# Attention by whole blocks of 128 queries instead of halves of 64, in a fused sliding-window trunk

## Chip, cores and metric

One core of one Trainium2 chip. The metric is the device time of one execution in microseconds (us), median of several runs. One execution is also recorded by the hardware profiler; its spans are measured from its first instruction.

Engines: PE is TensorE (matmul), DVE is VectorE, ACT is ScalarE, POOL is GpSimd, SP is SyncE, which issues most DMAs. PEld is PE's loading of stationary operands.

## What is computed

One layer of a trunk on 512 tokens of width 2048: an RMS norm, attention in a sliding window of 128 keys (32 heads of 64, 4 key/value heads, a relative bias by head, a sink per head in the softmax), a gate, the output projection, then a gated embedding and a last norm. In the reference, cut to the attention:

```python
qi, kj = np.arange(BLOCK)[:, None], np.arange(2 * BLOCK)[None, :]
dist = qi + BLOCK - kj
band = (dist >= 0) & (dist < WINDOW)
scores = einsum('bnqhgd,bnjhd->bnhgqj', q, kb) * HEAD_DIM ** -0.5 + bias
scores = where(mask, scores, finfo.min)
m = maximum(scores.max(-1), sink)
e = exp(scores - m)
probs = e / (e.sum(-1) + exp(sink - m))
out = einsum('bnhgqj,bnjhd->bnqhgd', probs, vb)
y = (out * silu(gate)) @ w_out
x = x + y
x = x + (p @ ple_proj) * sigmoid(rmsnorm(x) @ ple_gate)
return rmsnorm(x, final_g)
```

## The kernel before

Everything is float32 to the eye. To run PE at the rate of its reduced float32 (`F32R`) without losing digits, each operand is split into a high part (a cast on ACT) and a low part (a subtraction on DVE), and a product is three matmuls: high by high, high by low, low by high (`mm3`, L125 to L130).

The kernel has four stages. Up to about 72 us it loads x and the first weights and makes keys, values and the first two pairs of query heads. Then come the **projections** for the other queries and for the gates, 30 pieces ("kinds", L182 to L192) of 16 steps; a step is one `mm3`, three matmuls of 128 x 512. Attention is woven between these steps. From 453 us the output projection and the gated embedding follow, each by a seven-product scheme on quadrants. The last stretch has no matmul.

Attention goes over 8 groups of four heads (`TWOS`, index d) and, in each, over 8 **halves** of 64 queries (`UNITS`, index g); i counts the 64 of these. The 128 rows of a score tile are 4 heads by 32 queries, so a half needs two score products (u = 0, 1). Three functions, written as generators, hold a half's steps:

- `scores(i)` (L447): two products of Q with the keys (L463) into a PSUM tile `s` of two banks, 160 keys wide, high and low part of the key side by side; POOL puts the sink into the row; DVE adds the bias and the two parts (L488, L489), folds the keys that two of the rows don't share (L490) and takes the maxima (L492); ACT takes the exponentials and their sums (L496); DVE inverts the sums (L498); ACT scales (L507) into `pr`.
- `turn(i)` (L509): two transposes (L516) into a bank `pt`; ACT and DVE split it into high and low (L521, L522), which are `r`; from the second block of queries on POOL cuts out the triangle of the window (L532), and ACT puts the low part beside the high one (L542): `own`.
- `weigh(i)` (L544): two products with V (L558) and, from the second block on, one of `own` with differences of V (L560) into a bank `o`, which two halves share; after the second half ACT and DVE add its two parts into `u` (L569, L571).

The loop over i (L824) sets the order. In this stage no scheduler moves an instruction: PE, SP, DVE, ACT and POOL take them as written (L329). At the head of iteration i stand the transposes of half i-2, the products with V of half i-3 and the scores of half i, then about seven projection steps. Between these steps stand the later parts of the generators and **chores**: the splits of the next weights (`W.todo`, one slot an iteration; L111 on ACT, L112 on DVE), the evacuation of a finished projection (`evac_q`, L305, with splits L320 and L322; `open_gate`, L589), the splits of the next key (`make_key`, L341), the gating of finished heads (`gate_value`, L582), the triangles' differences (`first_chores`, L428). Two more DMA chains run through it: `sum_weights` (L641) has SP copy and POOL add blocks of later weights in DRAM, and `load_bias` (L439) fetches the next bias.

`q_at` (L182) places the queries' projections so that Q of group d is ready for half 8 d. PSUM has eight banks: two each for projections ("p"), `pt` ("t") and `o` ("o"), and one buffer of two banks for `s`.

Of the kernel before, what the change touches and what calls it, by code (L numbers as in the profile page):

```python
# [11 lines left out]
F32 = mybir.dt.float32  # L12
# [18 lines left out]
UNITS = S // HB  # L31
# [9 lines left out]
WARM = 24  # L41
PAD = 48
# [14 lines left out]
def trunk_kernel(ctx: ExitStack, tc: tile.TileContext, a: dict):  # L57
# [11 lines left out]
    others = {"s": banks_s.enter_context(tc.tile_pool(name="psum_s", bufs=2, space=PSUM))}  # L69
# [112 lines left out]
    q_at = {int(0.5 + 3.516 * (c // 2)) - 3 + c % 2: c for c in range(2, PAIRS)}  # L182
# [214 lines left out]
    spsum = mid.enter_context(tc.tile_pool(name="psum_w", bufs=1, space=PSUM))  # L397
# [7 lines left out]
    U, T, PT, O, gates, biases = {}, {}, {}, {}, {}, {}  # L405
# [41 lines left out]
    def scores(i):  # L447

        d, g = divmod(i, UNITS)
        if g == 4 and d + 1 < TWOS:
            load_bias(d + 1)
        key = K[d // 2]

        s_ps = spsum.tile([P, 2, S], F32, tag="w", name=f"s{i}")
        number = [min(2 * g + u + 1, 5) * QB for u in range(2)]
        for u in range(2):  # L460
            first, n = max(2 * g + u - 4, 0) * QB, number[u]
            st = Q[d][:, 2 * g + u].rearrange("p h q -> p (h q)")
            nc.tensor.matmul(s_ps[:, u, : 2 * n], st, key[:, :, first : first + n], start=True, stop=True)  # L463
        W = KEYS + 2
        t = apool.tile([P, 2, W], F32, tag="t", name=f"t{i}", bufs=3)
        at = t[:, 0, 0:1]

        def two(of, stride, n):
            return bass.AP(tensor=at.tensor, offset=at.offset + of, ap=[at.ap[0], [stride, 2], [1, n]])

        late = QB if g >= 2 else 0
        seen = [t[:, 0, 0 : P + 1], t[:, 1, 1 + late : P + 2 + late] if late else t[:, 1, 0 : P + 1]]
        both = two(0, W + 1 + late if late else W, P + 1)
        pr = [t[:, u, 1 + late * u : 1 + late * u + P] for u in range(2)]
        nc.gpsimd.tensor_copy(two(0, W + W - 1 if late else W, 1), sinkb[:, d : d + 1].unsqueeze(1).to_broadcast([P, 2, 1]))
        for u, n in enumerate(number):
            if n < P:
                nc.gpsimd.memset(t[:, u, 1 + n : 1 + P], MASKED)
        yield
        bias = biases[d][:, ::-1]  # L480
        if g < 2:
            for u, n in enumerate(number):
                nc.vector.tensor_add(t[:, u, 1 : 1 + n], s_ps[:, u, :n], bias[:, KEYS - n :])
            for u, n in enumerate(number):
                nc.vector.tensor_add(t[:, u, 1 : 1 + n], s_ps[:, u, n : 2 * n], t[:, u, 1 : 1 + n])
        else:
            x = t[:, :, 1 : 1 + KEYS]
            nc.vector.tensor_add(x, s_ps[:, :, :KEYS], bias.unsqueeze(1).to_broadcast([P, 2, KEYS]))  # L488
            nc.vector.tensor_add(x, s_ps[:, :, KEYS : 2 * KEYS], x)  # L489
            nc.vector.tensor_max(two(1, W + P, QB), t[:, :, 1 : 1 + QB], t[:, :, 1 + P : 1 + KEYS])  # L490
        sm = apool.tile([P, 24], F32, tag="sm", name=f"sm{i}", bufs=4)
        nc.vector.tensor_reduce(sm[:, 0:2], both, axis=AX.X, op=ALU.max, negate=True)  # L492
        yield
        for u in range(2):
            su = seen[u]
            nc.scalar.activation(su, su, AF.Exp, bias=sm[:, u : u + 1], accum_out=sm[:, 2 + u : 3 + u])  # L496
        yield
        nc.vector.reciprocal(sm[:, 4:6], sm[:, 2:4])  # L498
        yield

        T[i] = apool.tile([P, 2, P], F32, tag="pr", name=f"pr{i}", bufs=3)
        for u in range(2):
            out, src = T[i][:, u], pr[u]
            if late and (g + u) % 2:
                out = out.rearrange("p (h k) -> p h k", h=2)[:, ::-1]
                src = src.rearrange("p (h k) -> p h k", h=2)
            nc.scalar.mul(out, src, sm[:, 4 + u : 5 + u])  # L507

    def turn(i):  # L509


        d, g = divmod(i, UNITS)
        pr = T.pop(i)
        pt = bank(f"pt{i}", "t")[:, :256]
        for u in range(2):
            nc.tensor.transpose(pt[:, u * P : (u + 1) * P], pr[:, u, :], ident)  # L516

        r = apool.tile([P, 2, 256], F32R, tag="r", name=f"r{i}", bufs=2)
        rh, rl = (r[:, l].rearrange("p (h u q) -> p u h q", h=4, u=2) for l in range(2))
        src = pt.rearrange("p (u h q) -> p u h q", u=2, h=4)  # L520
# [3 lines left out]
        own = None  # L524
        if g >= 2:
            own = apool.tile([P, 2, 256], F32R, tag="own", name=f"own{i}", bufs=2)
            rows = slice(0, P) if g % 2 else slice(0, HB)
            flat = lambda v: v[rows].rearrange("p l (u q) -> p (l u) q", q=HB)


            sign = -1 if g % 2 else 1
            nc.gpsimd.affine_select(  # L532
                out=flat(own), in_=flat(r).bitcast(F32), pattern=[[0, 8], [sign, HB]], compare_op=ALU.is_ge, fill=0.0,
                base=-HB - 1 if g % 2 else 0, channel_multiplier=-sign,
            )
        PT[i] = (r, own)
        yield
        if own is not None:
            here, there = slice(HB, P), slice(0, HB)
            if g % 2 == 0:  # L540
                here, there = there, here
            nc.scalar.copy(own[there, 0], own[here, 1].bitcast(F32))  # L542

    def weigh(i):  # L544

        d, g = divmod(i, UNITS)
        n, b = divmod(g, 2)
        kv = d // 2
        r, own = PT.pop(i)
        if g == 0:  # L550
            U[d] = apool.tile([P, 2, S], F32, tag="u", name=f"u{d}", bufs=3)
        if b == 0:
            O[d] = bank(f"o{i}", "o").rearrange("p (b u e q) -> p b u e q", b=2, u=2, e=2)
        ops = O[d]
        out = ops[:, b].rearrange("p u e q -> p (u e q)")
        first = V[0 if n == 0 else n - 1 + b][:, kv]
        for low in range(2):
            nc.tensor.matmul(out, first, r[:, low], start=low == 0, stop=own is None and low == 1)  # L558
        if own is not None:
            nc.tensor.matmul(  # L560
                out, DV[:, n - 1, b, kv * 2 * HD : (kv + 1) * 2 * HD], own[:, 0], start=False, stop=True
            )
        yield
        if b:
            dst = U[d][:, :, n * P : (n + 1) * P].rearrange("p u (b q) -> p b u q", b=2)
            lower, upper = slice(0, 64), slice(64, 128)
            tmp = [apool.tile([P, 2, 2, HB], F32, tag=f"tmp{e}", name=f"tmp{e}_{i}", bufs=1) for e in range(2)]
            for e, (o, x) in enumerate(((lower, upper), (upper, lower))):
                nc.scalar.copy(tmp[e][o], ops[x, :, :, e, :])  # L569
            for e, o in enumerate((lower, upper)):  # L570
                nc.vector.tensor_add(dst[o], ops[o, :, :, e, :], tmp[e][o])  # L571
        if g == UNITS - 1:
# [243 lines left out]
    blocks = TWOS * UNITS  # L816
# [6 lines left out]
    softmax = iter(())  # L823
    for i in range(blocks + 3):  # L824
# [476 lines left out]
```

## Time and profile before

| what | value |
|---|---|
| median of 3 runs | 798.1 us (797.66 to 798.22) |
| the profiled execution, its own time | 798.39 us |
| its span, first to last instruction | 796.4 us |
| PE busy | 786.1 us |
| DVE, ACT, POOL busy | 586.9, 500.5, 117.4 us |
| mean granted clock of PE | 0.997 |

How to read it: a line of a group gives the source line, engine, operation, what is written from what, the shape, the count, and behind the bar the busy time, the mean duration of one in ns, and the idle time ahead of these instructions with what ended it. A line of the order in time gives start and duration in us. A matmul's duration reaches to the end of its result, and the next one starts before that; so durations of PE overlap, and its pace is read from starts. PE's weight load before each matmul is a row of its own (PEld).

### The profile page before, as it was taken

What the parts mean: (1) busy time and instruction counts of PE and PEld (TensorE: products, weight loads), DVE (VectorE), ACT (ScalarE), POOL (GpSimd) and SP (SyncE); (2) the same over time, 40 slices, a digit from 0 to 9 for tenths busy, and PEclk for the clock granted to TensorE, in tenths of its full rate; (3) what the DMA queues carried; (4) which work ended last, traced back from release to release, by engine and by line L of the source; (5) the groups of instructions that cost most, each with busy time, mean ns of one, the idle gap of its engine ahead of it and who ended that gap; (6) DMA issues with size and microseconds to landing.
All of it is one profiled execution on the core that took longest, in us unless ns stands there. A gap on an engine that the chain in (4) does not pass through costs nothing.

```text
span 796.4 us, 10979 instructions
## 1 busy us (share of the span) xinstructions
PE 786.1 (99%) x3758; PEld 658.4 (83%) x3758; DVE 586.9 (74%) x1026; ACT 500.5 (63%) x1057; POOL 117.4 (15%) x238
## 2 busy tenths in 40 slices
PE   9999999999999999999999999999999999999995
PEld 8888888888888888888888888888888888888884
DVE  4555697877878687777778898766646757988896
ACT  6652576666767586666657645555568656656765
POOL 0030223131212213121222100030000020200000
PEclk9999999999999999999999999999999999999998
DMA  9882389697869869777965478997613995787633
GB/s 352 260 243 92 113 261 236 174 255 179 223 178 255 204 192 241 188 220 171 260 156 150 118 267 328 356 256 235 204 34 103 374 212 197 155 225 220 206 106 106
DMA packets 42919, 165.28 MB, mean 208 GB/s; under 512 B 6048, under 2 KB 7072, under 8 KB 39024
## 3 DMA queue, kind: packets, MB, share of 16 engines
q1 hardware_dynamic: 35456, 129.67, 47.6%
q0 software_dynamic: 7408, 34.93, 23.6%
q8 instruction: 29, 0.48, 0.2%
q14 instruction: 26, 0.21, 0.1%
HBM read 157.70 MB, written 46.19 MB: 256 GB/s over the span
## 4 chain that ended last, share of the span: by engine, by line
PE 99%; DVE 0%; ACT 0%; issue 0%; ACTq 0%; DVEq 0%
PE gps L128 7%; PE gps L130 7%; PE gps L129 7%; PE qps L128 7%; PE qps L130 7%; PE qps L129 7%; PE o L128 6%; PE o L130 6%; PE o L129 6%; PE g L128 5%; PE g L129 5%; PE g L130 5%; PE s L463 2%; PE o L558 2%; PE vps L280 2%; PE pt L516 2%
## 5 line engine op out<-in xcount | busy, mean ns | idle before, releaser
L676 DVE TENSOR_TENSOR blo<-braw,bhi 128x1024 fp32r<-128x1024 f32 x80 | 97.7, 1221 | 40.0 <-ACT bhi L675 40.0
L675 ACT CAST bhi<-braw 128x1024 fp32r<-128x1024 f32 x80 | 84.1, 1052 | 65.6 <-PE g L130 21.7
L128 PE MATMUL gps<-xh,whi 128*128 128x512 f32 x256 | 99.9, 390 | 0.1
L130 PE MATMUL gps<-xh,wlo 128*128 128x512 f32 x256 | 99.8, 390 | 0.0
L129 PE MATMUL gps<-xl,whi 128*128 128x512 f32 x256 | 99.8, 390 | 0.0
L128 PE MATMUL o<-bhi,fho 128*128 128x512 f32 x224 | 87.7, 391 | 0.0
L128 PE MATMUL qps<-xh,whi 128*128 128x512 f32 x224 | 87.7, 391 | 0.0
L130 PE MATMUL qps<-xh,wlo 128*128 128x512 f32 x224 | 87.4, 390 | 0.0
L129 PE MATMUL qps<-xl,whi 128*128 128x512 f32 x224 | 87.4, 390 | 0.0
L129 PE MATMUL o<-blo,fho 128*128 128x512 f32 x224 | 87.2, 389 | 0.0
L130 PE MATMUL o<-bhi,flo 128*128 128x512 f32 x224 | 87.2, 389 | 0.0
L112 DVE TENSOR_TENSOR wlo<-wraw,whi 128x1024 fp32r<-128x1024 f32 x60 | 73.8, 1231 | 2.8 <-ACT whi L111 2.4
L128 PE MATMUL g<-bhi,fhg 128*128 128x512 f32 x192 | 75.1, 391 | 0.0
L130 PE MATMUL g<-bhi,flg 128*128 128x512 f32 x192 | 74.8, 389 | 0.0
L129 PE MATMUL g<-blo,fhg 128*128 128x512 f32 x192 | 74.7, 389 | 0.0
L532 POOL TENSOR_SCALAR_AFFINE_SELECT own<-r 64x512 fp32r<-64x512 f32 (+1 forms) x48 | 32.4, 675 | 254.8 <-DVE r L522 250.1
L521 ACT CAST r<-pt 128x256 fp32r<-128x256 f32 x64 | 23.8, 371 | 71.8 <-PE pt L516 71.5
L522 DVE TENSOR_TENSOR r<-pt,r 128x256 fp32r<-128x256 f32 x64 | 27.1, 423 | 55.7 <-ACT r L521 55.0
L111 ACT CAST whi<-wraw 128x1024 fp32r<-128x1024 f32 x60 | 62.3, 1040 | 5.3 <-issue 3.9
L676 DVE TENSOR_TENSOR blo<-grown,bhi 128x1024 fp32r<-128x1024 f32 x32 | 39.1, 1223 | 23.6 <-ACT bhi L675 23.4
L130 PEld LDWEIGHTS gps<-xh,wlo 128*128 128x128 f32 x256 | 48.1, 188 | 10.1
L128 PEld LDWEIGHTS gps<-xh,whi 128*128 128x128 f32 x256 | 48.1, 188 | 9.4 <-PE vps L280 0.5
(207 smaller groups left out, 1739.7 us busy)
## 6 DMA issues: line engine op xcount, KB each, us to landing
wraw<-in_w_gate_in SPq DMA_DIRECT2D x32, 512.0 KB, 5.5
wraw<-in_w_q SPq DMA_DIRECT2D x28, 512.0 KB, 4.6
w_out<-in_w_out POOLq DMA_DIRECT2D x24, 512.0 KB, 7.2
braw<-in_w_out SPq DMA_DIRECT2D x24, 512.0 KB, 4.3
braw<-in_ple_gate SPq DMA_DIRECT2D x24, 512.0 KB, 4.4
xw<-in_first SPq DMA_DIRECT2D x14, 640.5 KB, 6.4
w_out<-in_w_out SPq DMA_DIRECT2D x16, 512.0 KB, 6.0
ple_gate<-in_ple_gate SPq DMA_DIRECT2D x16, 512.0 KB, 6.7
```

Source lines behind the costliest of these rows:

```text
L111: nc.scalar.copy(hi, raw)
L112: nc.vector.tensor_sub(lo, raw, hi.bitcast(F32))
L128: nc.tensor.matmul(ps, sh, mh, start=first, stop=False, skip_group_check=more)
L129: nc.tensor.matmul(ps, sh, ml, start=False, stop=False, skip_group_check=more)
L130: nc.tensor.matmul(ps, sl, mh, start=False, stop=last, skip_group_check=more)
L280: nc.tensor.matmul(v_ps[t], h[:, c], both[:, :, 256:512], start=f, stop=e, skip_group_check=True)
L463: nc.tensor.matmul(s_ps[:, u, : 2 * n], st, key[:, :, first : first + n], start=True, stop=True)
L521: nc.scalar.copy(rh, src)
L522: nc.vector.tensor_sub(rl, src, rh.bitcast(F32))
L532: nc.gpsimd.affine_select(out=flat(own), in_=flat(r).bitcast(F32), pattern=[[0, 8], [sign, HB]], compare_op=ALU.is_ge, fill=0.0, base=-HB ...
L675: nc.scalar.copy(hi, raw)
L676: nc.vector.tensor_sub(lo, raw, hi.bitcast(F32))
```

## The change

The unit of attention becomes a block n of 128 queries: 32 units instead of 64. `scores` makes four products into a PSUM tile of four banks, and each DVE step of the softmax (adds, fold, maxima, reciprocals) and the split of the transposes is one instruction for four rows of heads instead of two. Exponentials, scalings, transposes, triangles, and the products with V are as many as before and of the same shapes. Four transposes go to one whole bank. In the first block of each group of heads the eight adds of narrow shapes stay apart.

The loop runs 34 times. At the head of iteration j stand, in this order, the scores of block j, the products with V of block j-2, the transposes of block j-1; then 13 or 14 projection steps, in two sevens (`HALF`) that carry the chores as an iteration did before. `t` and `o` lose their second bank, which `s` takes. The buffers of `pr`, `r`, `own` go from three, two, two to one of twice the size, `t` from three to two. `q_at` changes its step from 3.516 to 3.41, since 34 iterations divide the projections otherwise than 66; the first projection woven in is now a query piece.

```diff
-    others = {"s": banks_s.enter_context(tc.tile_pool(name="psum_s", bufs=2, space=PSUM))}
+    others = dict.fromkeys("sto", banks_s.enter_context(tc.tile_pool(name="psum_s", bufs=2, space=PSUM)))
...
-    q_at = {int(0.5 + 3.516 * (c // 2)) - 3 + c % 2: c for c in range(2, PAIRS)}
+    q_at = {int(0.5 + 3.41 * (c // 2)) - 3 + c % 2: c for c in range(2, PAIRS)}
...
-    spsum = mid.enter_context(tc.tile_pool(name="psum_w", bufs=1, space=PSUM))
+    spsum = mid.enter_context(tc.tile_pool(name="psum_w", bufs=1, space=PSUM, reuse_waits="tile"))
+    others.update(dict.fromkeys("to", spsum))
...
-        s_ps = spsum.tile([P, 2, S], F32, tag="w", name=f"s{i}")
-        number = [min(2 * g + u + 1, 5) * QB for u in range(2)]
-        for u in range(2):
-            first, n = max(2 * g + u - 4, 0) * QB, number[u]
-            st = Q[d][:, 2 * g + u].rearrange("p h q -> p (h q)")
-            nc.tensor.matmul(s_ps[:, u, : 2 * n], st, key[:, :, first : first + n], start=True, stop=True)
+        s_ps = spsum.tile([P, 4, S], F32, tag="w", name=f"s{i}")
+        number = [min(4 * n + v + 1, 5) * QB for v in range(4)]
+        for v in range(4):
+            first, c = max(4 * n + v - 4, 0) * QB, number[v]
+            st = Q[d][:, 4 * n + v].rearrange("p h q -> p (h q)")
+            nc.tensor.matmul(s_ps[:, v, : 2 * c], st, key[:, :, first : first + c], start=True, stop=True)
         W = KEYS + 2
-        t = apool.tile([P, 2, W], F32, tag="t", name=f"t{i}", bufs=3)
+        t = apool.tile([P, 4, W], F32, tag="t", name=f"t{i}", bufs=2)
...
-            nc.vector.tensor_add(x, s_ps[:, :, :KEYS], bias.unsqueeze(1).to_broadcast([P, 2, KEYS]))
+            nc.vector.tensor_add(x, s_ps[:, :, :KEYS], bias.unsqueeze(1).to_broadcast([P, 4, KEYS]))
             nc.vector.tensor_add(x, s_ps[:, :, KEYS : 2 * KEYS], x)
-            nc.vector.tensor_max(two(1, W + P, QB), t[:, :, 1 : 1 + QB], t[:, :, 1 + P : 1 + KEYS])
+            pairs = t.rearrange("p (b u) c -> p b u c", u=2)
+            nc.vector.tensor_max(four(1, W + P, QB), pairs[:, :, :, 1 : 1 + QB], pairs[:, :, :, 1 + P : 1 + KEYS])
...
-        nc.vector.reciprocal(sm[:, 4:6], sm[:, 2:4])
+        nc.vector.reciprocal(sm[:, 8:12], sm[:, 4:8])
...
-        T[i] = apool.tile([P, 2, P], F32, tag="pr", name=f"pr{i}", bufs=3)
+        T[i] = apool.tile([P, 4, P], F32, tag="pr", name=f"pr{i}", bufs=1)
...
-        pt = bank(f"pt{i}", "t")[:, :256]
-        for u in range(2):
-            nc.tensor.transpose(pt[:, u * P : (u + 1) * P], pr[:, u, :], ident)
-
-        r = apool.tile([P, 2, 256], F32R, tag="r", name=f"r{i}", bufs=2)
+        pt = bank(f"pt{i}", "t")
+        for v in range(4):
+
+            c = 2 * (v % 2) + v // 2
+            nc.tensor.transpose(pt[:, c * P : (c + 1) * P], pr[:, v, :], ident)
+        yield
+
+        r = apool.tile([P, 2, 512], F32R, tag="r", name=f"r{i}", bufs=1)
...
-        if b == 0:
-            O[d] = bank(f"o{i}", "o").rearrange("p (b u e q) -> p b u e q", b=2, u=2, e=2)
...
+        ops = bank(f"o{i}", "o").rearrange("p (b u e q) -> p b u e q", b=2, u=2, e=2)
+        for b in range(2):
+            out = ops[:, b].rearrange("p u e q -> p (u e q)")
+            first = V[0 if n == 0 else n - 1 + b][:, kv]
+            for low in range(2):
+                nc.tensor.matmul(
+                    out, first, r[:, low, 256 * b : 256 * b + 256], start=low == 0, stop=not n and low == 1
+                )
+            if n:
+                nc.tensor.matmul(
+                    out, DV[:, n - 1, b, kv * 2 * HD : (kv + 1) * 2 * HD], own[b][:, 0], start=False, stop=True
+                )
...
-    for i in range(blocks + 3):
...
+    for j in range(blocks + 2):
+
+        softmax = scores(j) if j < blocks else iter(())
+        turned = turn(j - 1) if 1 <= j <= blocks else iter(())
+        value = weigh(j - 2) if 2 <= j else iter(())
+        for part in (softmax, value, turned, softmax, turned):
+            next(part, None)
+        todo = left // (blocks + 2 - j)
         left -= todo
-        for n in range(max(todo, 6)):
+        for n in range(max(todo, 2 * HALF)):
+            h, at = divmod(n, HALF)
+            i = 2 * j + h
             if n < todo:
                 next(proj)
...
+            for part in {1: (turned,), 3: (softmax,), 5: (softmax, value), 6: (softmax,), 8: (turned,)}.get(n, ()):
+                next(part, None)
+            if at == HALF - 1 and h < 2 and j < blocks:
+                sums(i)
```

162 lines of the change are left out of this document (69 added, 93 removed).

## The prediction

> **What bounds the kernel now.** I read the page first: which engine is full, and when. Then the busy times by stage, which say whether the attention stage has any gap on TensorE that could be won.
>
> ```profile
> span 796.4 us, 10979 instructions
> PE 786.1 (99%) x3758; PEld 658.4 (83%) x3758; DVE 586.9 (74%) x1026; ACT 500.5 (63%) x1057; POOL 117.4 (15%) x238
> ```
>
> ```profile
> core 0: us, PE busy (x) PEld busy (x) DVE busy (x) ACT busy (x) POOL busy (x), PEclk, DMA share, GB/s
> 83.00:453.00 370.00, 370.00 (x1825) 311.23 (x1825) 284.78 (x625) 248.35 (x678) 80.84 (x173) 1.00 0.75 202
> ```
>
> Attention lies between about 83 and 453 us, interleaved with the projections. There PE is busy for 370.00 of 370.00 us at a granted clock of 1.00; DVE has 285 and ACT 248. So PE's stream of products sets the time, and DVE and ACT have 85 and 122 us to spare. What they save is worth nothing by itself; it only buys slack.
>
> The Trainium skill ("Perfetto Trace Analysis", "Identifying the Most-Contended Engine") says that matmul busy time is no good measure of PE's headroom, since matmuls are pipelined, and looks at weight loads instead; those stand at 311 of 370 us here. By that rule a full PE row is no proof. So I check the pace itself, on the order of PE's instructions in time (start, duration):
>
> ```profile
> 255.22 0.38 PE L516 MATMUL pt<-ident,pr 128*128 128x128 f32 x2
> 255.35 0.48 PE L558 MATMUL o<-r,V 128*128 128x256 f32 x2
> 255.67 0.28 PE L560 MATMUL o<-own,DV 128*128 128x256 f32 x1
> 255.79 0.46 PE L463 MATMUL s<-k,q 128*128 128x320 f32 x2
> 256.09 0.39 PE L128 MATMUL gps<-xh,whi 128*128 128x512 f32 x1
> 256.32 0.40 PE L129 MATMUL gps<-xl,whi 128*128 128x512 f32 x1
> 256.55 0.39 PE L130 MATMUL gps<-xh,wlo 128*128 128x512 f32 x1
> 256.78 0.39 PE L128 MATMUL gps<-xh,whi 128*128 128x512 f32 x1
> ...
> 260.64 0.39 PE L130 MATMUL gps<-xh,wlo 128*128 128x512 f32 x1
> 260.87 0.38 PE L516 MATMUL pt<-ident,pr 128*128 128x128 f32 x2
> ```
>
> Starts count here, since durations overlap. From 256.78 to 260.64 are 17 long products: 0.227 us each. One half (two transposes, three products with V, two scores) takes 256.09 - 255.22 = 0.87. From one half to the next are 260.87 - 255.22 = 5.65 us, and 0.87 + 21 x 0.227 = 5.64. So the whole price of a change between short and long products is what is left: 0.013 us a half, with rounded starts anything from 0.00 to 0.02. It is seen where it should be: the three long products after a half take 0.69 (256.09 to 256.78) for 0.68, the last before the next 0.23 for 0.227.
>
> **The change part by part.**
>
> *Products.* The instruction order of the changed kernel holds the same products: 128 scores, 128 transposes, 128 + 48 products with V and DV. They stand in 32 groups instead of 64 (with edge pieces 34 instead of 67): four scores, then four to six products with V, then four transposes. Cost of a full group: 4 scores at 0.15 (255.79 to 256.09 holds two) = 0.60; 6 products at 0.117 (255.67 to 255.79 and the rows above) = 0.70. Transposes in a longer row are shown in the output stage:
>
> ```profile
> 586.03 1.03 PE L938 MATMUL tp<-ident,x1s 128*128 128x128 f32 x8
> 586.83 0.48 PE L128 MATMUL o<-bhi,fho 128*128 128x512 f32 x1
> 587.14 0.40 PE L129 MATMUL o<-blo,fho 128*128 128x512 f32 x1
> ```
>
> 587.14 - 586.03 = 1.11 us less one long product of 0.23 leaves 0.88 for eight, 0.11 each; four are 0.44. Sum 0.60 + 0.70 + 0.44 = 1.74, which is 2 x 0.87. Inside the group nothing is won. What goes are 33 changes. At 0.02 us they are **-0.66 us**. The bounds are nothing (0.00 a change) and -0.7; a loss would need a longer group to be dearer than its pieces, for which no row speaks. I take 0.02, the upper end, since late starts show on both sides of a half.
>
> *Waits of PE.* Score tiles grow to four banks in one buffer; the transposes' bank and that of the products with V fall from two to one. Each is cleared early. DVE reads the scores at the head of a block and they come again one block (10.6 to 11.3 us) later; the V bank is evacuated by the middle of a block, some 5 us ahead of its next use. First use: the scores need four banks, which also held the values of the start:
>
> ```profile
> 79.75 0.48 DVE L373 SCALAR_TENSOR_TENSOR values<-vps,rstd,values 128x256 f32<-128x256 f32 x1
> ```
>
> ```profile
> 82.78 0.33 PE L463 MATMUL s<-k,q 128*128 128x64 f32 x2
> ```
>
> The last of these values leaves its bank at 80.2, the first scores start at 82.8: 2.5 us of cover. Cost of the banks: zero; a bank that came too late would show as a gap ahead of a group.
>
> *The softmax chain* is where it can get tight: a block's transposes come one block after its scores, where a half's came two halves after. That is the same 11 us, but twice the rows pass in it, step by step, and the transposes of all four wait for the last. (From transposes to V products the time grows, from a half to a block.) These rows price it, by shape over the stage (mean ns behind the bar), and ACT's pace from its instructions in time:
>
> ```profile
> L112 DVE TENSOR_TENSOR wlo<-wraw,whi 128x1024 fp32r<-128x1024 f32 x56 | 68.4, 1222 | 1.1 <-ACT whi L111 0.7
> L111 ACT CAST whi<-wraw 128x1024 fp32r<-128x1024 f32 x56 | 58.2, 1039 | 3.9 <-issue 3.9
> L522 DVE TENSOR_TENSOR r<-pt,r 128x256 fp32r<-128x256 f32 x64 | 27.1, 423 | 55.7 <-ACT r L521 55.0
> L492 DVE TENSOR_REDUCE sm<-t 128x2 f32<-128x258 f32 x64 | 27.0, 422 | 3.3
> L521 ACT CAST r<-pt 128x256 fp32r<-128x256 f32 x64 | 23.8, 371 | 71.8 <-PE pt L516 71.5
> L489 DVE TENSOR_TENSOR t<-s,t 128x320 f32<-128x320 f32 x48 | 23.6, 492 | 1.7
> L488 DVE TENSOR_TENSOR t<-s,bias 128x320 f32<-128x320 f32 x48 | 23.0, 480 | 0.0
> L542 ACT CAST own<-own 64x256 fp32r<-64x256 f32 x48 | 19.4, 404 | 4.7 <-POOL own L532 4.2
> L322 ACT CAST q<-qps 64x512 fp32r<-64x512 f32 x28 | 16.3, 580 | 13.9 <-DVE qps L313 13.7
> L490 DVE TENSOR_TENSOR t<-t 128x64 f32<-128x64 f32 x48 | 10.8, 225 | 1.6
> L483 DVE TENSOR_TENSOR t<-s,bias 128x128 f32<-128x128 f32 x8 | 2.2, 280 | 0.0
> ```
>
> ```profile
> 250.25 0.70 ACT L507 ACTIVATE pr<-t,sm 128x128 f32<-128x128 f32 x2
> 250.84 1.04 ACT L111 CAST whi<-wraw 128x1024 fp32r<-128x1024 f32 x1
> ...
> 252.39 0.75 ACT L569 COPY tmp<-o 64x256 f32<-64x256 f32 x2
> ...
> 253.47 0.41 ACT L496 ACTIVATE t<-t,sm 128x129 f32<-128x129 f32 x1
> 253.78 0.19 ACT L496 ACTIVATION_READ_ACCUMULATOR t<-t,sm 128x1 f32 x1
> 253.88 0.39 ACT L496 ACTIVATE t<-t,sm 128x129 f32<-128x129 f32 x1
> ```
>
> Each further column costs DVE (480 - 280) / 192 = 1.04 ns, so an add of 640 columns is an estimated 0.81 us (bounds 0.48, as one old instruction, and 0.98, as two), the second 0.83, the maximum 0.29, the sum's reduction 0.69 (bounds 0.42 and 0.84). Count from the start T of the group. Scores done T + 0.8; DVE through the reduction T + 3.4. ACT meanwhile waits for the transposes (T + 1.9), splits them (0.5) and a weight piece (1.0): T + 3.4. Four exponentials at the pace 0.41 (253.47 to 253.88): T + 5.1. DVE in that time subtracts the split (0.69) and a weight piece (1.22), so the reciprocal stands at T + 5.5. ACT evacuates V products (0.75), scales four rows at 0.30 (250.25 to 250.84): T + 7.1; then a weight piece 1.0 and two copies of "own" 0.8: **T + 8.9**. They are due at the next group: "own" after four scores and two products, T + 10.6 + 0.8 = T + 11.4 in the blocks of 13 projection steps (13 x 3 x 0.227 + 1.76 = 10.6), T + 12.1 in those of 14; the scaled rows at T + 11.9 or later. Cover 2.5 us. Chores of other work stand ahead in some blocks: a split of Q adds 2 x 0.58 on ACT, a key as much, since its copies have the same shape (64x512); the block with both is at T + 11.2, just inside. So the chain costs nothing, with little over in the fullest blocks.
>
> *DVE and ACT* lose half of their instructions per block, with their fixed part, some 0.15 us each (0.280 less 128 x 0.00104): hidden behind PE, zero in the sum. POOL has the same 48 selections, and DMA the same 284 issues on SP; the weights of the projections come in a slightly changed order (Q's turns come up to one projection earlier, 3.41 apart instead of 3.52), each of the same size: zero.
>
> *Sum.* The profiled execution took 798.39 us (span 796.4 and 2.0 around it), 0.3 over the median of 798.1. 798.39 - 0.66 = 797.7; on the median's footing **797.4**.
>
> **The rivals.**
>
> *The chain comes late (slower).* Place: ACT's copy of "own" and scaled rows, PE waiting in the middle of a group. It decides from T + 11.4 on: 2.5 us more than my sum in a plain block, 0.2 in the fullest. For it: DVE and ACT each have over 8 us of work in such a block, the waits between them go back and forth four times, and each step now waits for twice the rows ahead of it. Against: before, PE never waited in this stage. Price: a quarter us in each of the 24 blocks with "own" is 6 us: 803.4; half a us in every block 16 us: 813. The Trainium skill ("Perfetto Trace Analysis", "Optimizing Scalar/DVE Operations") speaks against the change here: engines that are not saturated but hold others up do better with smaller instructions, done sooner; DVE's 285 of 370 us is such a case, and the trace of before shows no hold-up. Chance 0.23.
>
> *Half the clock (slower).* Short products twice as long on end could let the clock fall. At half the clock for as long as a group lasts, 32 x 1.75 = 56 us: 853. Against: the granted clock (third figure from the end) over the eight transposes in a row is 1.00.
>
> ```profile
> 586.00:587.20 1.20, 1.20 (x11) 1.12 (x10) 0.00 (x0) 0.92 (x1) 0.00 (x0) 1.00 0.00 0
> ```
>  The Trainium skill ("TensorE: Matmul & The Clock Gate", "Part 4: PE-mode transpose") says that transposes do not count as busy for the clock; the trace does not show a drop after them. Chance 0.03.
>
> *Transposes pay per row, not per piece (faster).* After a row of transposes the next product's successor is late by 0.08 (255.35 holds two products for 0.32, where 0.24 is their pace). If that were the price of a row, 33 rows fewer save 2.6 us: 795.5. Against: eight in a row at 0.11 each, so each pays for itself. Chance 0.08.
>
> **How the numbers follow.** Forecast 797.4 with 0.66; late chain 0.23, clock 0.03, cheaper rows 0.08. About 0.2% (1.6 us) is what a measurement of this kernel can tell from no change: 796.5 to 799.7 is "same". Faster 0.08, from the cheaper rows; same 0.66, the forecast; slower 0.26, from the late chain and the clock. The forecast's own range is 797.0 to 798.1. For 8 in 10 the range takes in all of that and the late chain up to 803.4, and leaves out the longer delays, the clock and the cheapest rows: 796.6 to 803.4.
>
> **What would show it.** In the changed profile: PE busy over the whole stage again, groups of 1.74 us, blocks 10.6 and 11.3 us apart. Right: the 3 to 5 ns of late starts 34 times. The late chain: gaps on PE ahead of L572 or L526 in the new numbering, released by ACT. Wrong in the premise: the granted clock below 1.00, or longer products after a group than 0.23.

## The result and the profile after

| | before | after |
|---|---|---|
| median | 797.97 us (797.66 to 798.22, 6 runs) | 800.9 us (800.43 to 801.83, 6 runs) |
| ratio | | 1.0036 (95%: 1.0026 to 1.0047) |
| profiled execution, its own time | 798.39 us | 800.75 us |
| its span | 796.4 us | 798.8 us |
| attention stage, worked out below | 380.92 us | 384.02 us |

The changed kernel is slower by 0.36%, some 2.9 us, where 0.66 us less was forecast. The page of the changed kernel, its engines:

```profile
PE 786.9 (99%) x3758; PEld 661.3 (83%) x3758; DVE 571.2 (72%) x858; ACT 496.2 (62%) x1025; POOL 130.8 (16%) x206
```

DVE lost 168 of its 1026 instructions and 15.7 us, ACT 32 of 1057 and 4.3 us; that the two lose half of their instructions per block, as the prediction has it, is too much, but its sum took nothing from it. The busy times of the stage, changed kernel (columns: length, then busy time of each engine, then clock):

```profile
83.00:456.00 373.00, 371.22 (x1824) 314.63 (x1823) 271.21 (x462) 245.35 (x650) 94.01 (x141) 1.00 0.73 201
```

PE was busy for 370.00 of 370.00 us before; now 1.8 us are missing, at the same granted clock of 1.00. The waits of PE in that window name what it stood for (total, times, longest):

```profile
PE o L572 <- ACT own L554: 1.8, 2, 1.3
```

**How long the stage is.** It runs from the first projection product behind the values to the first product of the output stage. In the order of PE's instructions of the kernel before, and then of the changed one:

```profile
71.80 0.47 PE L128 MATMUL gps<-xh,whi 128*128 128x512 f32 x1
...
452.72 0.40 PE L128 MATMUL o<-bhi,fho 128*128 128x512 f32 x1
```

```profile
71.29 0.47 PE L129 MATMUL qps<-xh,whi 128*128 128x512 f32 x1
...
455.31 0.39 PE L129 MATMUL o<-bhi,fho 128*128 128x512 f32 x1
```

452.72 - 71.80 = 380.92, 455.31 - 71.29 = 384.02: 3.1 us more. The stages behind it are as long as before (output stage 157.7, gate 148.8). A long product is a matmul of 128x512, as in the projections; the group is the row of short ones (scores, products with V, transposes) between them; a gap is the time from one product's start to the next one's. From the starts of all PE products in the stage, the 3.1 us split into three parts: **+2.77** inside three groups that are longer than their like (3.33, 1.87 and 2.44 us instead of 1.67, 1.52 and 1.67); **+0.52** in late starts of the long products from the second behind a group on (every gap less 0.22667 us, summed, with 0.08 behind the stage's first product: 1.40 instead of 0.88); and **-0.20** in all that is left, the groups themselves and the first long product behind each.

**The two large waits.** PE in order of time (the third, 0.35 us at 124.8, is under the bound of the waits view):

```profile
112.54 0.40 PE L568 MATMUL o<-r,V 128*128 128x256 f32 x2
114.28 0.39 PE L572 MATMUL o<-own,DV 128*128 128x256 f32 x1 [1.33 <-ACT own L554]
...
288.09 0.40 PE L568 MATMUL o<-r,V 128*128 128x256 f32 x2
288.94 0.39 PE L572 MATMUL o<-own,DV 128*128 128x256 f32 x1 [0.44 <-ACT own L554]
```

Between V products and own product are 1.74 and 0.85 us, where 0.24 is the pace. The block whose chain ends late at 112 began its group at T = 101.56. DVE and ACT of the changed kernel in that block (in brackets: idle time before, and what ended it):

```profile
102.42 1.23 DVE L113 TENSOR_TENSOR wlo<-wraw,whi 128x1024 fp32r<-128x1024 f32 x1 [3.69 <-ACT whi L112]
103.67 1.39 DVE L321 TENSOR_TENSOR q<-qps,q 64x512 fp32r<-64x512 f32 x2
...
105.88 0.82 DVE L492 TENSOR_TENSOR t<-s,bias 128x640 f32<-128x640 f32 x1
...
107.93 0.69 DVE L497 TENSOR_REDUCE sm<-t 128x4 f32<-128x516 f32 x1
...
111.19 0.86 DVE L582 TENSOR_TENSOR u<-o,tmp 64x256 f32<-64x256 f32 x2
```

```profile
101.35 1.04 ACT L112 CAST whi<-wraw 128x1024 fp32r<-128x1024 f32 x1
...
108.71 0.40 ACT L503 ACTIVATE t<-t,sm 128x129 f32<-128x129 f32 x1 [3.59 <-DVE sm L497]
...
111.28 1.28 ACT L515 ACTIVATE pr<-t,sm 128x128 f32<-128x128 f32 x4
112.46 0.39 ACT L362 CAST V<-values 128x256 fp32r<-128x256 f32 x1
112.76 1.04 ACT L112 CAST whi<-wraw 128x1024 fp32r<-128x1024 f32 x1
113.82 0.83 ACT L554 CAST own<-own 64x256 fp32r<-64x256 f32 x2
```

DVE comes to the additions at T + 4.3, not at T + 0.8: it stood 3.7 us for a weight cast of the block before, which ACT reached late, and has splits of Q and V ahead of the additions. ACT then stands 3.6 us for the maxima, and own ends at T + 13.1. In the block of 288 (T = 276.42), ACT:

```profile
282.38 1.18 ACT L323 CAST q<-qps 64x512 fp32r<-64x512 f32 x2 [2.71 <-DVE qps L314]
...
285.92 1.28 ACT L515 ACTIVATE pr<-t,sm 128x128 f32<-128x128 f32 x4
287.21 1.25 ACT L353 CAST k<-kt 64x512 fp32r<-64x512 f32 x2
288.48 0.83 ACT L554 CAST own<-own 64x256 fp32r<-64x256 f32 x2
```

This is the block with a split of Q and a key. ACT sits idle for 2.71 us in it, because Q's scaling stands on DVE behind additions, maxima and splits; own ends at T + 12.9.

### The profile page after: what moved, and what is told of

It reads as the page before. It is cut to its first block, busy times and chain, and to the rows that moved or that the text cites. A ratio compares the mean times of both kernels' runs of the same rounds, so it can differ in the third digit from the quotient of the medians.

```text
span 798.8 us, 10755 instructions
## 1 busy us (share of the span) xinstructions
PE 786.9 (99%) x3758; PEld 661.3 (83%) x3758; DVE 571.2 (72%) x858; ACT 496.2 (62%) x1025; POOL 130.8 (16%) x206
## 4 chain that ended last, share of the span: by engine, by line
PE 92%; ACT 3%; DVE 3%; issue 1%; DMA 1%; ACTq 0%; DVEq 0%
PE o L131 6%; PE o L129 6%; PE qps L129 6%; PE o L130 6%; PE qps L131 6%; PE qps L130 6%; PE gps L129 6%; PE gps L131 6%; PE gps L130 6%; PE g L131 5%; PE g L129 5%; PE g L130 5%; PE vps L281 2%; PE s L465 2%; PE o L568 2%; PE pt L526 2%
## 5 line engine op out<-in xcount | busy, mean ns | idle before, releaser
L129 PE MATMUL gps<-xh,whi 128*128 128x512 f32 x256 | 101.5, 396 | 0.0
L543 POOL TENSOR_SCALAR_AFFINE_SELECT own<-r 64x512 fp32r<-64x512 f32 (+1 forms) x48 | 53.4, 1132 | 253.2 <-DVE r L533 253.2
L532 ACT CAST r<-pt 128x512 fp32r<-128x512 f32 x32 | 18.8, 588 | 71.1 <-PE pt L526 70.9
L503 ACT ACTIVATE t<-t,sm 128x129 f32<-128x129 f32 x128 | 50.0, 393 | 15.2 <-DVE sm L497 14.7
L130 PEld LDWEIGHTS gps<-xl,whi 128*128 128x128 f32 x256 | 48.1, 188 | 9.5
```

The source lines that it names most:

```text
L129: nc.tensor.matmul(ps, sh, mh, start=first, stop=False, skip_group_check=more)
L130: nc.tensor.matmul(ps, sh, ml, start=False, stop=False, skip_group_check=more)
L503: nc.scalar.activation(sv, sv, AF.Exp, bias=sm[:, v : v + 1], accum_out=sm[:, 4 + v : 5 + v])
L532: nc.scalar.copy(rh, src)
L543: nc.gpsimd.affine_select(out=both(own[b]), in_=both(r[:, :, 256 * b : 256 * b + 256]).bitcast(F32), pattern=[[0, 2], [0, 4], [sign, HB]], ...
```

## The experiments

Theory A: the loss is the late chain, as these two blocks show it. Its rivals in the first runs were P, that POOL is late with its selections (1.13 us each on the mean instead of 0.67), and G, that the longer groups cost by themselves. From the run with the own copies on POOL on, P stands for another rival: a crowded block has too much work in whatever order, and a piece moved ahead makes another late. Late starts are given as the sum defined above, the stage in the same way as above; the medians of the kernel before beside the runs were 797.8 to 798.0.

**Own copies ahead of the weight cast** (theory A against P and G).

```diff
-{1: (turned,), 3: (softmax,), 5: (softmax, value), 6: (softmax,), 8: (turned,)}
+{1: (turned,), 3: (softmax,), 5: (softmax, value), 6: (softmax, turned)}
```

> The two copies of "own" on ACT stand right behind the four scalings of the block instead of behind the next weight split, the chores of the second seven steps and a key. Theory A (the 2.9 us are three blocks in which ACT brings "own" late; ACT's order decides): the wait at 112.6 us shrinks from 1.5 to about 0.2, those at 124.8 (0.17) and 288.2 (0.6) go; 800.9 falls by 2.3 to 2.8 us, to about 798.2. Rival P (POOL is late: its selections take 1.1 us on the mean instead of 0.68): the copies now wait for POOL, the scalings behind them no sooner, and the time stays within 0.5 us of 800.9. Rival G (the longer groups themselves cost): 800.9 stays, since the groups are the same.

Measured 802.28 us (802.11 to 803.15), ratio 1.0054 [1.0041, 1.0066]; stage 385.4. Slower than the change itself, which none of the three readings had. The waits of PE:

```profile
PE o L572 <- ACT own L554: 0.9, 3, 0.3
PE o L568 <- DVE u L582: 0.7, 1, 0.7
PE o L568 <- ACT pr L515: 0.2, 1, 0.2
```

The longest wait for own fell from 1.3 to 0.3, but others came. With own first, the weight cast comes later, DVE's half of that weight piece with it, and the additions of the next block behind it. Here that block began at 199.59, its additions at T + 3.5:

```profile
200.53 1.23 DVE L113 TENSOR_TENSOR wlo<-wraw,whi 128x1024 fp32r<-128x1024 f32 x1 [2.39 <-ACT whi L112]
...
203.08 0.82 DVE L492 TENSOR_TENSOR t<-s,bias 128x640 f32<-128x640 f32 x1
```

So a shift inside ACT's queue only moves the lateness: the end of one block's queue is the head of the next one's. This is where the second rival P comes from. POOL's selections, as slow as in the changed kernel (1.12 us on the mean), end at 111.85 in the block of 112, and ACT's copies begin at 112.76: POOL was not what they waited for.

**Q's places as before** (is the new spacing of Q at fault?).

```diff
-    q_at = {int(0.5 + 3.41 * (c // 2)) - 3 + c % 2: c for c in range(2, PAIRS)}
+    q_at = {int(0.5 + 3.516 * (c // 2)) - 3 + c % 2: c for c in range(2, PAIRS)}
```

> One part undone: the query projections stand where they stood before (step 3.516), so the first woven projection is a gate again and the first block's chain has no split of Q ahead of its exponentials. Theory A, with the late start due to the Q split and table load in the first block: the waits of the blocks at 112 and 125 us (2.0 us with what follows them) shrink to under 0.5, the one at 288 may move; time about 799.2. Rival (the start is late because of the small splits of V and its differences alone): nothing moves, 800.9.

Measured 806.33 us (805.37 to 807.56), ratio 1.0102 [1.0088, 1.0116]; both readings on record missed. Its waits of PE:

```profile
PE s L465 <- DVE q L321: 3.8, 2, 2.3
PE o L572 <- ACT own L554: 2.3, 3, 1.3
```

The new spacing is needed: with the old one Q itself is late by up to 2.3 us. And the waits for own stay with the old one too.

**The last key one group of heads later** (the block at 288 alone).

```diff
-                if i in (6, 20, 36):
-                    idle.extend(make_key(1 + i // 16))
+                if i in (6, 20, 44):
+                    idle.extend(make_key({6: 1, 20: 2, 44: 3}[i]))
```

> The fourth key is made eight half-blocks later, in a block without a split of Q. Theory A: only the wait at 288 us goes (0.61 and two late starts of 0.1): 800.9 falls by 0.8 to 800.1. Rival P or G: no change, since POOL and the groups are as they were.

Measured 800.17 us (799.7 to 800.77), ratio 1.0026 [1.0017, 1.0036]; stage 383.30. One wait is left, the one at 112 (1.3 us); the block at 288 waits no more. Its price was thus 0.7 us, as theory A had it; P and G had no change.

**Without the split of the transposes.** Left out are ACT's cast and DVE's subtraction on the transposes; selections and V products work on one constant tile.

```diff
-        r = apool.tile([P, 2, 512], F32R, tag="r", name=f"r{i}", bufs=1)
...
-        nc.scalar.copy(rh, src)
-        nc.vector.tensor_sub(rl, src, rh.bitcast(F32))
+        r = still
...
```

> Leaves out the split of the transposes (ACT's and DVE's reading of that bank) and uses one constant tile in its place; everything else stands. Question: why did the late starts of long products not halve with the groups (38 ns behind each group now, 20 ns twice before)? Theory C (they come from ACT and DVE working on the transposes and scores at that moment, so they go with the work): the first four long products behind a group fall from 233 ns to 227-229. Rival D (they are PE's own, after a run of short products): 233 ns stay. Time about 798 to 800, as the chain is shorter.

Measured 799.05 us (one run); stage 382.60, late starts 1.28 instead of 1.40. The second to fourth long product behind a group take 232.1 ns on the mean instead of 233.0, so rival D is right here: the reads of the transposes' bank carry only 0.1 us of the late starts.

**Own copies on POOL**, right behind the selections (takes ACT's queue out of the chain without moving anything in it).

```diff
-            nc.scalar.copy(own[b][there, 0], own[b][here, 1].bitcast(F32))
+            nc.gpsimd.tensor_copy(own[b][there, 0], own[b][here, 1].bitcast(F32))
...
-{1: (turned,), 3: (softmax,), 5: (softmax, value), 6: (softmax,), 8: (turned,)}
+{1: (turned, turned), 3: (softmax,), 5: (softmax, value), 6: (softmax,)}
```

> The two copies of the own rows go from ACT to POOL, right behind the selects that they read. Theory A (the 2.9 us that the changed kernel lost are three waits of TensorE for these copies, which stand last in ACT's order behind exponentials, scalings and a weight cast): the copies end about 6 us after the group's start instead of 12, no wait for them is left, and neither the block whose key and Q splits meet nor the two at the start of the stage wait: 798.0 (797.6 to 798.5), level with the kernel before. Rival P (crowded blocks shift their lateness to the next piece in the chain, as when the copies were put ahead of the weight cast on ACT): waits for the scaled rows or the output additions come in their place, 799.5 to 802. Rival L (POOL's work beside VectorE's slows VectorE or is slowed by it, 1.58 us for a select instead of 0.65): the copies end after 11 us, and the time is 801 or more.

Measured 798.63 us (797.78 to 799.8), ratio 1.0010 [1.0001, 1.0019]; stage 381.67. In the block of 112, POOL's order in time:

```profile
108.75 2.38 POOL L543 TENSOR_SCALAR_AFFINE_SELECT own<-r 64x512 fp32r<-64x512 f32 x2 [16.51 <-DVE r L533]
111.20 0.85 POOL L554 CAST own<-own 64x256 fp32r<-64x256 f32 x2
```

Own ends at 112.05 even there, and no wait for it is left: 2.34 us of the 3.09 are back, as theory A said (the time is 0.1 over its range). L fell, and P all but fell: of the waits that it names, one of 0.34 us came. 0.75 us stay: these 0.34 in the group at 122, where the products with V start at 122.80 and DVE's additions (L582), which clear their bank, end at 122.66; late starts 1.45 instead of before's 0.88 (+0.57); and the rest -0.16.

**DVE's softmax in halves inside the block** (is the size of the instructions at fault?).

```diff
...
+        for b in range(2):
+            c = slice(2 * b, 2 * b + 2)
...
+                nc.vector.tensor_add(x, s_ps[:, c, :KEYS], bias.unsqueeze(1).to_broadcast([P, 2, KEYS]))
+                nc.vector.tensor_add(x, s_ps[:, c, KEYS : 2 * KEYS], x)
+                nc.vector.tensor_max(two(1, W + P, QB), t[:, c, 1 : 1 + QB], t[:, c, 1 + P : 1 + KEYS])
...
+            nc.vector.tensor_reduce(
...
```

> Only VectorE's work on the scores is undone: the additions, the fold and the reduction run for each half of a block by itself, so that the first half's exponentials can start some 1.2 us earlier; VectorE gets 4 instructions more in a block. Theory A: the waits at the start of the stage shrink from 1.7 to about 0.5 us, the wait at 288 (where ACT stood for Q's scaling) stays: 799.3 to 800.0. Rival S (the size of these instructions is no part of the loss; ACT's own queue is): the waits stay and the time is 800.7 to 801.5.

Measured 805.68 us (804.86 to 805.74), ratio 1.0095 [1.0081, 1.0108]: both theories missed, and by 4.8 us over the change itself. The same block, DVE and ACT (ACT's own copies are L561 in this kernel):

```profile
106.33 0.49 DVE L502 TENSOR_TENSOR t<-s,bias 128x320 f32<-128x320 f32 x1
...
109.28 0.42 DVE L505 TENSOR_REDUCE sm<-t 128x2 f32<-128x258 f32 x1
```

```profile
108.16 0.41 ACT L510 ACTIVATE t<-t,sm 128x129 f32<-128x129 f32 x1 [3.10 <-DVE sm L505]
...
109.73 0.40 ACT L510 ACTIVATE t<-t,sm 128x129 f32<-128x129 f32 x1 [0.69 <-DVE sm L505]
...
114.89 0.83 ACT L561 CAST own<-own 64x256 fp32r<-64x256 f32 x2
```

The additions start 0.45 us later, since the block before ended later in the same way. The first exponential still starts 0.55 us earlier (108.16 for 108.71), but the second half's maxima are done later: DVE needs 109.70 - 106.33 = 3.37 us for both, where the whole block took 108.62 - 105.88 = 2.74. ACT stands 0.69 us in the middle and 0.95 us more for the reciprocals (L512), which stand behind the second half on DVE; own begins 1.07 us later. The chain waits for its last instruction, so halves only add to it. The size of DVE's instructions on the scores is no part of the loss; it keeps the loss small.

**Without DVE's work on the scores.** Left out are additions, fold and maxima; the exponentials work on constant rows.

```diff
-            nc.vector.tensor_add(x, s_ps[:, :, :KEYS], bias.unsqueeze(1).to_broadcast([P, 4, KEYS]))
...
-        nc.vector.tensor_reduce(
...
+        sm = marks
...
```

> Left out: VectorE's additions of bias and halves, the fold and the reduction; the exponentials work on constant rows, so the output isn't the reference's. Theory C (the late starts of the long products after a group come from VectorE reading the scores' banks beside TensorE): positions 3 to 10 after a group fall from a mean of 231 ns to 227, some 1.0 us over 32 groups, and with the waits gone too (chain 3 us earlier) the time is 796.5 to 797.2. Rival D (they are TensorE's own, whatever the others do): the positions keep their 231 ns, and only the waits go: 797.8 to 798.3.

Measured 797.14 us (one run); stage 381.03. The time lies in theory C's range, but its mechanism falls: the two large waits are gone, as both theories said (the group at 285 is still 0.34 us longer than its like), and the late starts are still 1.28, where the changed kernel has 1.40 and the one with the own copies on POOL 1.45. DVE's reads of the scores carry 0.1 to 0.2 us of them.

**The group in three places** and **the group in the order of the kernel before**, both with the own copies on POOL. In the first, a projection step of three long products stands behind the scores and another behind the outputs; in the second:

```diff
-        for part in (softmax, value, turned, softmax, turned):
+        for part in (turned, value, softmax, turned, softmax):
```

> On the kernel with the own copies on POOL, which has no wait left and whose attention stage is still 0.75 us longer than before's (late starts of long products after a group 1.45 us in sum instead of 0.88, and 0.19 in the groups): the group's 14 short products stand in three places with three long products between them (scores, then outputs, then transposes). Theory G (each change between long and short products costs by itself, as the prediction had it at 0.02 us): 64 changes more, 799.6 to 800.2. Theory B (a long row of short products is what makes the next ones late): the late starts fall below 1.0 us in sum, 797.9 to 798.3. Theory N (they come with neither): 798.4 to 798.9.

> On the same kernel: the group in the order that the kernel before has (transposes, outputs, scores; the split ahead of the additions on VectorE). Theory O (which products stand last before the long ones, and which reads of their banks follow, makes the late starts): they fall from 1.45 us in sum to about 0.5, 797.8 to 798.2. Theory B and theory N: they stay at 1.4, 798.4 to 798.9; a chain that starts its exponentials 0.7 us later has cover for it now that the own copies are early, so no wait comes back.

Three places: 799.05 us (798.58 to 800.49), ratio 1.0016 [1.0007, 1.0025], between the ranges of N and G; stage 382.52, late starts 1.42. The late starts don't follow the length of a row of short products, so B falls. G falls too: the 62 changes more between short and long products cost nearly nothing, since of the 0.85 us of stage 0.8 is one wait of another kind, for DVE's additions that clear the bank of the products with V:

```profile
PE o L568 <- DVE u L582: 0.8, 1, 0.8
```

Order of before: late starts **0.55**, as theory O said. But 801.34 us (800.89 to 801.83), ratio 1.0039 [1.0027, 1.0052], stage 384.64, where O had 797.8 to 798.2: the part of the expectation that no wait comes back was wrong. The transposes now open the group and wait for the scaled rows. PE at 112:

```profile
112.62 1.21 PE L526 MATMUL pt<-ident,pr 128*128 128x128 f32 x4
113.60 0.47 PE L568 MATMUL o<-r,V 128*128 128x256 f32 x2
```

Four transposes take 0.98 us from start to start, where 0.35 is the pace (255.09 to 255.44 below). They come 1.3 us sooner, and with the split ahead of the additions on DVE the rows come later.

**Transposes between scores and outputs**, own copies on POOL.

```diff
-        for part in (softmax, value, turned, softmax, turned):
+        for part in (softmax, turned, value, softmax, turned):
```

> On the kernel with the own copies on POOL: in the group the transposes stand between scores and outputs, so that the outputs, whose bank nobody reads for some 6 us, stand last. Theory O (the late starts, 1.45 us in sum with the transposes last and 0.55 with the scores last, follow from the products ahead of the long ones): they fall to 0.5 to 0.9. The scaled rows are due 0.75 us earlier; their least room in the kernel on which this one stands was 0.44 and 0.73 us, in two blocks at the stage's start, so at most 0.4 us of waiting comes back: 798.0 to 798.6. Theory N (the late starts belong to the length of the group): they stay at 1.4 and the time is 798.7 to 799.2.

Measured 797.53 us (796.4 to 798.69), ratio 0.9996 [0.9987, 1.0005]. Late starts **0.31**, stage **380.16**: 0.77 us shorter than before, the only version with that. Late starts and time are below what theory O gave (0.5 to 0.9, 798.0 to 798.6). One group, at 122, still loses 0.54 us, since its transposes wait for the scaled rows; without that the stage would be 1.3 us shorter. One block of the changed kernel, from its transposes to the eleventh long product behind them, then the same of this one, whose group ends with the outputs:

```profile
255.09 0.60 PE L526 MATMUL pt<-ident,pr 128*128 128x128 f32 x4
255.44 0.49 PE L129 MATMUL qps<-xh,whi 128*128 128x512 f32 x1
255.76 0.40 PE L130 MATMUL qps<-xl,whi 128*128 128x512 f32 x1
...
257.85 0.39 PE L130 MATMUL qps<-xl,whi 128*128 128x512 f32 x1
```

```profile
253.10 0.40 PE L129 MATMUL qps<-xh,whi 128*128 128x512 f32 x1
253.34 0.39 PE L130 MATMUL qps<-xl,whi 128*128 128x512 f32 x1
...
255.38 0.39 PE L130 MATMUL qps<-xl,whi 128*128 128x512 f32 x1
```

The second to the eleventh long product take 2.09 us in the one and 2.04 in the other, 9 x 0.2267. In time this version can't be told from the kernel before: the stretch behind the last product's start was 10.7 us in its profiled execution, 9.6 in before's, and a profile of each is all there is for that.

**The same, with V's splits spread over five blocks.**

```diff
     def first_chores(i, step):
+        i = {0: 0, 2: 1, 3: 2, 5: 3, 6: 4, 8: 5}.get(i, -1)
+        if i < 0:
+            return
```

> The same, and the splits of V and of its differences, which crowd the first three blocks, are spread over the first five. Theory A (crowding at the start is what makes the chain late there): the scaled rows' room at the stage's start grows by 1 us or more, no wait is left, 797.6 to 798.2, a little under or level with before. Rival P: the pieces that are moved crowd the fourth and fifth block instead, whose room is 2.4 us, and waits come there: 798.5 or more.

Measured 799.54 us (798.89 to 801.86), ratio 1.0023 [1.0015, 1.0032], in rival P's range and over theory A's. A piece that was moved came late itself, not the chain. PE at 112:

```profile
115.58 0.47 PE L571 MATMUL o<-r,V 128*128 128x256 f32 x2 [1.93 <-DVE V L363]
```

I had put V's second block half a block ahead of its first use, and DVE did not get there in time. All other groups of the stage have their regular length, so the scaled rows are in time everywhere else, as theory A said; what better places for V would give was not run.

**The order alone**: the changed kernel with transposes between scores and outputs, own copies on ACT. The edit is the one line shown under "Transposes between scores and outputs".

> The changed kernel with the transposes ahead of the outputs in its group and nothing else: the own copies stay on ACT. If the two causes add up, the stage loses 1.1 us of late starts and 0.4 in the groups, and the three waits for own rows (2.9 us), which are due 0.4 us later now, shrink by 0.4 us each or to nothing, to about 1.7: attention 381.3 to 381.8 instead of 384.0, and 798.0 to 798.8 in all, level with before within 0.1%. If the late starts fall only where no wait is, or the transposes now wait for the scaled rows: 799.5 or more.

Measured 798.96 us (798.16 to 800.08), ratio 1.0016 [1.0007, 1.0025]; stage 381.71, inside its forecast, the time 0.2 over it. Late starts 0.37, and in three groups 2.1 us of waits instead of 2.8, of which the waits view shows the largest:

```profile
PE o L572 <- ACT own L554: 0.9, 1, 0.9
```

So the two causes stand side by side: the order is worth 1.0 in late starts and 0.6 in the groups, whether own waits or not, and own's lateness comes on top.

## Why the prediction was wrong, step by step

- **PE's stream sets the time**: right as far as the runs tell. The stage, read from PE's starts, lengthened and shortened with the time; what lies outside it took 416.1 to 417.8 us in the profiled executions, so that the time alone can't show a difference under a microsecond.
- **"33 changes at 0.02 us are -0.66 us"**: failed in the changed kernel, where groups and late starts together are +0.32 (0.52 - 0.20). What the step left out is the order inside the group, which the change also turned: transposes first before, last after. In that order a group makes the next ten long products late. With the transposes in the middle, groups are -0.73 and late starts -0.57, 1.3 us in all (less the one wait of 0.54 in that run). In the order of the kernel before, late starts are 0.55 instead of 0.88, while waits hide the rest. So half as many groups save late starts in both of these orders, and the place of the transposes took the saving away. Nor was it the change between short and long products that cost 0.02: 62 more of those came for nearly nothing.
- **Waits for banks cost zero**: right in the changed kernel, whose profile has no wait for one. But the cover of the V bank, "some 5 us", was not there in every block: at the start of the stage the additions that clear it (L582, shown above) end at 112.05, 0.49 us ahead of the next product with V (112.54). Three of the runs waited once for this bank in the waits view (own copies earlier 0.7 us, softmax in halves 0.6, group in three places 0.8), and the own copies on POOL lost 0.34 us to it.
- **"The chain costs nothing", own ready at T + 8.9**: this step made the kernel slower, +2.77 us. In plain blocks it holds. The terms of DVE were right in size: 0.81, 0.83, 0.29 and 0.69 forecast; the changed kernel, by shape:

```profile
L497 DVE TENSOR_REDUCE sm<-t 128x4 f32<-128x516 f32 x32 | 22.1, 692 | 1.7
L493 DVE TENSOR_TENSOR t<-s,t 128x640 f32<-128x640 f32 x24 | 19.8, 825 | 0.8
L492 DVE TENSOR_TENSOR t<-s,bias 128x640 f32<-128x640 f32 x24 | 19.8, 825 | 17.8 <-PE s L465 17.6
```

  What failed is the way of adding. For the fullest block, "T + 11.2, just inside", I summed ACT's work and left out the 2.71 us in which ACT stands for Q's scaling; it came to T + 12.9. And each block was counted from its own T with idle engines, while at the stage's start DVE still works on the block before and begins at T + 4.3. That block, with V's splits in it, I had not looked at.
- **The rival "The chain comes late"** named the right place, ACT's copy of own, and the right sign. Its price was wrong: three blocks are late, by 0.4 to 1.7 us, not all 24 by a quarter. It is only through this rival that 800.9 lies inside the wide range of 796.6 to 803.4; the forecast's own 797.0 to 798.1 missed it. The Trainium skill ("Perfetto Trace Analysis", "Optimizing Scalar/DVE Operations") says that smaller instructions may get work done sooner when an unsaturated engine holds others up, which the prediction put as a rule without the "may"; here, with DVE's work on the scores in halves, they did not, and the kernel took 805.68 us.
- **The rival "Transposes pay per row"** (faster) was dismissed for a wrong reason: that eight in a row go at 0.11 each says nothing of the products behind them. With the transposes in the middle the 1.3 us fit a price of 0.04 for each of the 33 rows of transposes fewer (it was put at 0.08); that it is these rows and nothing else that comes half as often is argued, not shown.
- **Half the clock**: no; 1.00 over the stage.

Open: why long products start late behind transposes. It is not the reads of the transposes' bank nor DVE's work on the scores (0.1 us, and 0.1 to 0.2), nor the length of the row of short products; only the order changed it, from 1.45 to 0.55 and 0.31.

## What to carry to other kernels

When a chain of engines is given half as many turns, don't count it from an idle start: lay out the block in which the extra work stands with every engine's queue from the block before, and let each step begin at the later of its input and its engine's place. A small copy at the end of a full queue can be moved to an engine that is idle: here that gave back 2.3 us of the stage, while moving it ahead in the same queue cost 1.4, since the next piece came late. And in a full PE stream the order of short products can matter as much as how often they come: here, moving the transposes from the end of a group to its middle was worth 1.6 to 1.7 us of the stage, though no run shows why.

## What was not expected of the hardware

**POOL's selections beside DVE.** The selections are the same 48 of the same shapes. Groups of the kernel before, then of the changed one (mean ns behind the bar):

```profile
L532 POOL TENSOR_SCALAR_AFFINE_SELECT own<-r 128x512 fp32r<-128x512 f32 x24 | 16.7, 697 | 100.5 <-DVE r L522 95.8 <-DMA wraw<-in_w_gate_in 4.7
L532 POOL TENSOR_SCALAR_AFFINE_SELECT own<-r 64x512 fp32r<-64x512 f32 x24 | 15.7, 652 | 154.3 <-DVE r L522 154.3
```

```profile
L543 POOL TENSOR_SCALAR_AFFINE_SELECT own<-r 64x512 fp32r<-64x512 f32 x24 | 35.2, 1468 | 253.2 <-DVE r L533 253.2
L543 POOL TENSOR_SCALAR_AFFINE_SELECT own<-r 128x512 fp32r<-128x512 f32 x24 | 19.1, 797 | 0.0
```

In the changed kernel the first selection of a pair mostly meets DVE's subtraction of a weight piece, both of whose inputs lie in SBUF. The 22 selections that do take 1.58 us in the median, the others 0.66. Before, none met that one; a single one, at 449 us, met such a subtraction of the output's weights and took 1.58 us too. The Trainium skill ("SBUF — State Buffer", "Who interferes with whom") says that a DVE instruction with two inputs in SBUF contends with a POOL instruction that reads SBUF; these runs agree, and put 0.9 us on it. DVE's subtraction took 1.22 us with and without. It cost nothing here, as the run with the own copies on POOL shows: own was ready in time even behind slow selections.

**Small late starts.** The late starts, some 40 ns in all over the ten long products behind a row of transposes, are too small for a view of waits; only the starts of hundreds of products, added up, show them. Between the transposes at the end of the group and in its middle they differ by 1.1 us of 800.
